# Lower halves of all expert-table blocks on VectorE, gathers paced by a one-column copy, first modulation columns turned in place

## Chip, core and metric

One core of a Trainium2 chip runs the whole program in one launch. The metric is the device time of that launch in microseconds (us). TensorE (PE), VectorE (DVE), ScalarE (ACT), GpSimd (POOL) and the queues of SyncE (SP) work side by side and wait for each other by semaphores.

## The reference, cut to what matters

Two layers, each a token mixer followed by a mixture of 16384 single-neuron experts ("PEER"). The mixture picks 16 experts for each of 8 heads of a token, by product keys:

```python
def peer_ffn(h, w_q, sub_keys, u_tab, v_tab):      # per block of 128 tokens
    s = einsum('thpd,hpnd->thpn', (xb @ w_q).reshape(t, 8, 2, 128), sub_keys)
    s_top, i_top = top_k(s, 16)
    c_top, c_idx = top_k(s_top[:, :, 0, :, None] + s_top[:, :, 1, None, :], 16)
    expert, gate = i1 * 128 + i2, softmax(c_top)
    act = gelu(einsum('td,thkd->thk', xb, u_tab[expert]))
    return einsum('thk,thkd->td', gate * act, v_tab[expert])
```

Before each mixer the input is normalized and modulated by a shift and a scale that come from one matrix product with `ada_w` (SEQ 512, context 256, D_MODEL 1024, float32 throughout).

## The kernel before, in words

**Two ways to the experts.** For three of the four tiles of 128 latent tokens (`ND = 3`, 384 tokens) the kernel works densely: all 16384 experts, in 128 blocks of 128 rows of each table, with a gate that is zero where an expert was not chosen (`peer_dense`, names `xp_` in layer 0, `yp_` in layer 1). For the fourth latent tile, and for the two context tiles of layer 0 (`cp_`), it fetches the chosen rows by indirect DMA from POOL, 128 rows of 4 KB a time (`gather_slots`, L1227), and DVE multiplies them: `jk` (L1245) for rows of `u`, `acc` (L1256) for rows of `v`. A gather needs one of six row buffers, and DVE's product gives it back. Layer 0 has 768 gathers, layer 1 has 256.

**Dense block.** Matrix products run in three passes on a rounded upper part and a remainder of each operand. For block b, SP loads `ur` (512 KB) and `vr` (512 KB), and every fourth block `gb` (768 KB of gates), each into two buffers. ACT rounds `ur` to `uh` (L1346) and `vr` to `vh` (L1384); the remainders `ul = ur - uh` (L1347) and `vl = vr - vh` are subtractions over 128x1024. PE forms the scores `sp` in 24 matmuls, ACT applies gelu (`ge`), DVE multiplies by the gates (`a`, L1394), ACT rounds to `ah`, DVE subtracts to `al` (L1399), and PE adds to the six accumulators `acc` in 18 matmuls. In program order the scores of block b stand ahead of the accumulation of block b-1.

**Who subtracts.** `ul` is on POOL for all 100 blocks that compute scores here. `vl` is on DVE for these (L1388) and on POOL for the last 28 (`FILL`, L1386), whose scores were computed earlier in the routing stage and are loaded as `gel`.

**Pacing.** `load(b)` ends with `pump(anchor, k)`: it writes the next k gathers into the program (3 a block in layer 0, 2.5 in layer 1, 2 in FILL) and puts each behind `anchor` on POOL. The anchor is the POOL subtraction of that block. Gathers and their products have the lowest priority, so a scheduler puts them where it expects idle time. In other stages `tick` (L1290) does the pacing: a copy of one column on POOL, which is then the anchor. What is left of the gathers after layer 0's dense stage is paced by ticks in layer 1's mixer and drained there.

**Start.** `ada` forms the modulation rows `ar`, writes them to memory (L179), `ada_cols(0)` reads them back as `ac_r` (L194), PE turns them in four transposes, and DVE copies the result to `cols` (L198), which ACT needs for the first normalized input `c_hT` (L235).

Of the kernel before, what the change touches and what calls it, by code (L numbers as in the profile page):

```python
# [9 lines left out]
F32 = mybir.dt.float32  # L10
# [9 lines left out]
P = 128  # L20
# [7 lines left out]
FILL = range(P - 28, P)  # L28
# [12 lines left out]
class Trunk:  # L41
# [114 lines left out]
    def ada(self, pool, layer, groups, ps):  # L156


        nc = self.nc
        for g in groups:  # L160
# [9 lines left out]
            b = pool.tile([P, 512], F32, tag="ab", name="ab" + nm)  # L170
            nc.sync.dma_start(b, self.I["ada_b"][layer, g])
            r = pool.tile([P, 512], F32, tag="ar", name="ar" + nm, bufs=2)
            nc.vector.tensor_add(r, acc, b)
            if g != 1:
# [14 lines left out]
    def ada_cols(self, layer):  # L189

        self.cols = self.rowpool.tile([P, 4, P], F32, tag="cols", name="cols")
        with self.tc.tile_pool(name=f"ac{layer}", bufs=1) as pool:
            r = pool.tile([P, 512], F32, name=f"ac_r{layer}")
            self.nc.sync.dma_start(r, self.rowd[layer][0])  # L194
            pt = self.ps("cols_ps")
            for b in range(4):
                self.tr(pt[:, b * P:(b + 1) * P], r[:, b * P:(b + 1) * P])
            self.nc.vector.tensor_copy(self.cols, pt)  # L198

# [1138 lines left out]
    def expert_scores(self, pool, b, xT, layer, nm, ps):  # L1338
# [7 lines left out]
        nc.scalar.copy(uh, uv)  # L1346
        anchor = nc.gpsimd.tensor_sub(ul, uv, uh)  # L1347

# [11 lines left out]
    def peer_dense(self, xs, xT, up, layer, nm, done):  # L1360
# [3 lines left out]
        with ExitStack() as st:  # L1364
# [4 lines left out]
            def load(b):  # L1369
# [95 lines left out]
    def build(self):  # L1465
        nc, tc, I = self.nc, self.tc, self.I
        with ExitStack() as st:
# [13 lines left out]
            with ExitStack() as l0:  # L1481
# [175 lines left out]
```

## Time and profile before

| | us |
|---|---|
| median of 3 runs (4374.13 to 4380.30) | 4376.23 |
| the profiled execution | 4360.89 |
| its span, first to last instruction | 4359.1 |
| PE busy | 3943.7 (90%) |
| DVE busy | 3497.9 (80%) |
| POOL busy | 2035.1 (47%) |
| layer 0, dense stage (first to last `sp`/`acc` matmul) | about 1553 to 2567 |
| layer 1, dense stage | about 3380 to 4342 |

The share of an engine over the whole span mixes stages with different limits, so the dense stages are read in windows: a stretch in which PE is busy for all its length is bound by PE, and only a stretch in which it is not can be shortened from outside. "Busy" for PE is a modelled end of a pipelined matmul; block times are therefore read from the start of one block's matmuls to the start of the next.

### The profile page before, as it was taken

To read this page: it belongs to the slowest core of one execution; us is meant where nothing else is said; L and a number is where in the kernel's file an instruction comes from. 1 tells how busy PE (TensorE), PEld (TensorE's weight loads), DVE (VectorE), ACT (ScalarE), POOL (GpSimd) and SP (SyncE) were. 2 spreads that over 40 slices of the span, in tenths; PEclk is the share of its full clock that TensorE was granted. 3 is DMA by queue.
4 is the path that set the end of the run, shared out by engine and by line. 5 is a ranking of instruction groups with operands and counts; after the bars stand their busy time and mean duration, and the time that the engine had idled before them with its cause. 6 is when DMAs were issued, how large, how long until landed. Compare 5 with 4: busy or idle time off the path is not lost.

```text
span 4359.1 us, 58568 instructions
## 1 busy us (share of the span) xinstructions
PE 3943.7 (90%) x20450; PEld 3198.6 (73%) x20450; DVE 3497.9 (80%) x6787; ACT 1613.3 (37%) x2929; POOL 2035.1 (47%) x1467
## 2 busy tenths in 40 slices
PE   7998888887799979999999865999999999999998
PEld 4676554685476767999999653775767899999986
DVE  1355989998899979999999977553998888888886
ACT  2353443353124523333333231562245333333333
POOL 0003367555630078767666856001200766666664
PEclk8999998998899989999999987999999999999999
DMA  8825498867934699999999978203246988888885
GB/s 305 295 105 158 166 323 315 279 222 242 316 118 159 227 365 353 346 344 352 337 345 332 325 260 301 67 26 103 73 161 232 346 317 308 309 305 312 309 287 178
DMA packets 484855, 1113.89 MB, mean 256 GB/s; under 512 B 38736, under 2 KB 256336, under 8 KB 475344
## 3 DMA queue, kind: packets, MB, share of 16 engines
q1 hardware_dynamic: 328896, 561.75, 37.4%
q0 software_dynamic: 147600, 537.40, 34.3%
q10 hardware_dynamic: 8064, 11.01, 0.7%
q8 instruction: 161, 2.64, 0.2%
q14 instruction: 134, 1.10, 0.1%
HBM read 1036.56 MB, written 73.92 MB: 255 GB/s over the span
## 4 chain that ended last, share of the span: by engine, by line
PE 61%; DVE 20%; DMA 8%; issue 6%; ACT 2%; POOL 2%; SPq 0%; DVEq 0%; ACTq 0%; POOLq 0%
PE yp_acc L75 10%; PE yp_sp L75 10%; PE xp_sp L75 9%; PE xp_acc L75 8%; PE mq_s L75 2%; DVE cp_acc L1256 2%; DMA cp_u<-peer_u,cp_idx 2%; PE x_p L75 1%; DVE cp_jk L1245 1%; PE yp_pg L75 1%; PE xp_pg L75 1%; DVE xp_acc L1256 1%; PE ada_ps L75 1%; PE yp_qy L75 1%; PE c_p L75 1%
## 5 line engine op out<-in xcount | busy, mean ns | idle before, releaser
L1227 POOL DMA_INDIRECT cp_u<-peer_u,cp_idx x256 | 318.0, 1242 | 316.0 <-DVE cp_jk L1245 222.6
L1347 POOL TENSOR_TENSOR yp_ul<-yp_ur,yp_uh 128x1024 fp32r<-128x1024 f32 x100 | 242.0, 2420 | 421.1 <-ACT yp_uh L1346 421.0
L75 PE MATMUL xp_sp<-xp_xT,xp_uh 128*128 128x384 f32 x1600 | 409.7, 337 | 12.4 <-ACT xp_uh L1346 12.4
L75 PE MATMUL yp_sp<-yp_xT,yp_uh 128*128 128x384 f32 x1600 | 408.8, 336 | 1.4 <-ACT yp_ge L1453 1.4
L1227 POOL DMA_INDIRECT cp_v<-peer_v,cp_idx x256 | 317.3, 1239 | 164.4 <-DVE cp_acc L1256 100.0
L75 PE MATMUL xp_acc<-xp_vh,xp_al 128*128 128x512 f32 x768 | 309.1, 402 | 31.9 <-DVE xp_al L1399 31.9
L1256 DVE SCALAR_TENSOR_TENSOR cp_acc<-cp_v,cp_act,cp_acc 128x1024 f32<-128x1024 f32 x254 | 330.9, 1303 | 6.9 <-DMA cp_v<-peer_v,cp_idx 4.4
L1394 DVE TENSOR_TENSOR yp_a<-yp_ge,yp_gb 128x384 f32<-128x384 f32 x100 | 237.3, 2373 | 123.3 <-ACT yp_ge L1356 123.3
L75 PE MATMUL xp_acc<-xp_vh,xp_ah 128*128 128x512 f32 x768 | 304.9, 397 | 15.8 <-ACT xp_ah L1398 15.8
L1347 POOL TENSOR_TENSOR xp_ul<-xp_ur,xp_uh 128x1024 fp32r<-128x1024 f32 x100 | 249.6, 2496 | 130.0 <-ACT xp_uh L1346 129.5
L75 PEld LDWEIGHTS xp_sp<-xp_xT,xp_uh 128*128 128x128 f32 x1600 | 293.2, 189 | 20.6 <-ACT xp_uh L1346 13.0
L75 PE MATMUL yp_acc<-yp_vh,yp_al 128*128 128x512 f32 x768 | 302.5, 394 | 5.5 <-DVE yp_al L1399 5.5
L75 PE MATMUL xp_acc<-xp_vl,xp_ah 128*128 128x512 f32 x768 | 304.8, 397 | 0.0
L75 PE MATMUL yp_acc<-yp_vl,yp_ah 128*128 128x512 f32 x768 | 301.6, 393 | 2.6 <-POOL yp_vl L1386 2.6
L75 PE MATMUL yp_acc<-yp_vh,yp_ah 128*128 128x512 f32 x768 | 299.9, 390 | 2.7 <-ACT yp_ah L1398 2.7
L75 PEld LDWEIGHTS yp_sp<-yp_xT,yp_uh 128*128 128x128 f32 x1600 | 292.4, 188 | 9.7 <-ACT yp_ge L1453 2.0
L75 PE MATMUL yp_sp<-yp_xT,yp_ul 128*128 128x384 f32 x800 | 269.4, 337 | 3.2 <-POOL yp_ul L1347 3.2
L75 PE MATMUL xp_sp<-xp_xT,xp_ul 128*128 128x384 f32 x800 | 269.8, 337 | 1.4 <-POOL xp_ul L1347 1.4
L1394 DVE TENSOR_TENSOR xp_a<-xp_ge,xp_gb 128x384 f32<-128x384 f32 x100 | 206.3, 2063 | 45.7 <-ACT xp_ge L1356 45.7
L1057 POOL TENSOR_TENSOR yp_wql<-yp_wq,yp_wqh 128x1024 fp32r<-128x1024 f32 x16 | 38.7, 2420 | 369.1 <-DMA yp_wq<-peer_w_q 311.5
L1346 ACT CAST yp_uh<-yp_ur 128x1024 fp32r<-128x1024 f32 x100 | 105.2, 1052 | 270.5 <-issue 214.7
L1398 ACT CAST xp_ah<-xp_a 128x384 fp32r<-128x384 f32 x128 | 65.8, 514 | 367.7 <-DVE xp_a L1394 323.5
(1479 smaller groups left out, 10753.1 us busy)
## 6 DMA issues: line engine op xcount, KB each, us to landing
xp_ur<-peer_uT SPq DMA_DIRECT2D x128, 512.0 KB, 5.7
xp_vr<-peer_v SPq DMA_DIRECT2D x128, 512.0 KB, 6.1
yp_ur<-peer_uT SPq DMA_DIRECT2D x128, 512.0 KB, 4.8
yp_vr<-peer_v SPq DMA_DIRECT2D x128, 512.0 KB, 4.9
aw<-ada_w SPq DMA_DIRECT2D x48, 1024.0 KB, 7.0
gdram<-xp_go SPq DMA_DIRECT2D x12, 2048.0 KB, 6.9
xp_gb<-gdram SPq DMA_DIRECT2D x32, 768.0 KB, 9.2
gdram<-yp_go SPq DMA_DIRECT2D x12, 2048.0 KB, 7.0
```

The lines of the kernel that those rows point to most:

```text
L75: self.nc.tensor.matmul(out, lhsT, rhs, start=start, stop=stop)
L1057: self.pump(nc.gpsimd.tensor_sub(wl, raw, wh), 0)
L1227: d = nc.gpsimd.indirect_dma_start(out=r, out_offset=None, in_=tab, in_offset=bass.IndirectOffsetOnAxis(ap=idx[:, j:j + 1], axis=0))
L1245: return nc.vector.scalar_tensor_tensor(junk, u, 1.0, h2, op0=ALU.mult, op1=ALU.mult, accum_out=act[:, j:j + 1])
L1256: i = nc.vector.scalar_tensor_tensor(acc, v, act[:, j:j + 1], acc, op0=ALU.mult, op1=ALU.add)
L1346: nc.scalar.copy(uh, uv)
L1347: anchor = nc.gpsimd.tensor_sub(ul, uv, uh)
L1394: nc.vector.tensor_mul(a.rearrange("p (g t) -> p g t", t=32), ge.rearrange("p (g t) -> p g t", t=32), gbs[b // 4][:, :, b % 4, :])
L1398: nc.scalar.copy(ah, a)
```

## The change

Three edits. Every `ul` and `vl` is subtracted on DVE. The gathers of the dense stage are paced by `tick(vh)`, a POOL copy of one column of the block's `vh`; it is written only while gathers are left. And the first modulation rows are turned by PE straight from `ar`, without the way through memory (the write to memory stays, other stages read it).

```diff
@@ ada
             nc.sync.dma_start(self.rowd[layer][g], r)
+            if not (layer or g):
+                self.turn_cols(r)
...
+    def turn_cols(self, r):
+        self.cols = self.rowpool.tile([P, 4, P], F32, tag="cols", name="cols")
+        pt = self.ps("cols_ps")
+        for b in range(4):
+            self.tr(pt[:, b * P:(b + 1) * P], r[:, b * P:(b + 1) * P])
+        self.nc.vector.tensor_copy(self.cols, pt)
@@ expert_scores
-        anchor = nc.gpsimd.tensor_sub(ul, uv, uh)
+        anchor = nc.vector.tensor_sub(ul, uv, uh)
@@ peer_dense, load
                 nc.scalar.copy(vh, vr)
-                if b in FILL:
-                    anchor = nc.gpsimd.tensor_sub(vl, vr, vh)
-                else:
-                    nc.vector.tensor_sub(vl, vr, vh)
-                self.pump(anchor, self.rate[layer] if b not in FILL else 2)
+                nc.vector.tensor_sub(vl, vr, vh)
+                self.tick(vh, self.rate[layer] if b not in FILL else 2)
                 return go, vh, vl
@@ build
                         weave(self.ada(ap, 0, (0,), self.ps))
-                        self.ada_cols(0)
```

POOL's queue in the first blocks of layer 0's dense stage, before: five gathers (`cp_u`) between the subtractions of blocks 6 and 7.

```order
L1347 TENSOR_TENSOR xp_ul6_12846<-xp_ur6_12843,xp_uh6_12845 128x1024
L1227 DMA cp_u1_109_12486<-peer_u0,cp_idx1_3839 128x1024
L1227 DMA cp_u1_110_12553<-peer_u0,cp_idx1_3839 128x1024
L1227 DMA cp_u1_111_12557<-peer_u0,cp_idx1_3839 128x1024
L1227 DMA cp_u1_112_12561<-peer_u0,cp_idx1_3839 128x1024
L1227 DMA cp_u1_113_12628<-peer_u0,cp_idx1_3839 128x1024
L1347 TENSOR_TENSOR xp_ul7_12921<-xp_ur7_12918,xp_uh7_12920 128x1024
```

The same place on POOL in the changed program, from the tick of block 6 to that of block 7.

```order
L1295 CAST tick_12861<-xp_vh6_12857 128x1
L1232 DMA cp_u1_109_12484<-peer_u0,cp_idx1_3833 128x1024
L1232 DMA cp_u1_110_12553<-peer_u0,cp_idx1_3833 128x1024
L1232 DMA cp_u1_111_12557<-peer_u0,cp_idx1_3833 128x1024
L1232 DMA cp_u1_112_12561<-peer_u0,cp_idx1_3833 128x1024
L1295 CAST tick_12938<-xp_vh7_12934 128x1
```

The subtraction has left POOL, and four gathers stand in a block where five stood; up to block 13 both programs place 56 gathers in the stage (1, 3, 1, 5, 4, 5, 5, 4, 5, 5, 4, 4, 5, 5 before; 4, 1, 4, 5, 4, 4, 4, 5, 4, 4, 4, 5, 4, 4 now), blocks 14 to 16 hold 4 or 3 of them before and 4 now, and from there on both have 3 a block.

DVE's queue in the middle of the stage, before: one block, from the gate product of block 41 to that of block 42.

```order
L1394 TENSOR_TENSOR xp_a41_15442<-xp_ge41_15440,xp_gb40_15328 128x384
L1256 SCALAR_TENSOR_TENSOR cp_acc1_13007<-cp_v1_101_15412,cp_act1_7245,cp_acc1_13007 128x1024
L1399 TENSOR_TENSOR xp_al41_15445<-xp_a41_15442,xp_ah41_15444 128x384
L1256 SCALAR_TENSOR_TENSOR cp_acc1_13007<-cp_v1_102_15478,cp_act1_7245,cp_acc1_13007 128x1024
L1256 SCALAR_TENSOR_TENSOR cp_acc1_13007<-cp_v1_103_15481,cp_act1_7245,cp_acc1_13007 128x1024
L1388 TENSOR_TENSOR xp_vl43_15547<-xp_vr43_15544,xp_vh43_15546 128x1024
L1394 TENSOR_TENSOR xp_a42_15514<-xp_ge42_15512,xp_gb40_15328 128x384
```

The same block on DVE in the changed program.

```order
L1396 TENSOR_TENSOR xp_a41_15520<-xp_ge41_15518,xp_gb40_15402 128x384
L1352 TENSOR_TENSOR xp_ul43_15621<-xp_ur43_15618,xp_uh43_15620 128x1024
L1401 TENSOR_TENSOR xp_al41_15523<-xp_a41_15520,xp_ah41_15522 128x384
L1390 TENSOR_TENSOR xp_vl43_15627<-xp_vr43_15624,xp_vh43_15626 128x1024
L1261 SCALAR_TENSOR_TENSOR cp_acc1_13019<-cp_v1_101_15490,cp_act1_7239,cp_acc1_13019 128x1024
L1261 SCALAR_TENSOR_TENSOR cp_acc1_13019<-cp_v1_102_15558,cp_act1_7239,cp_acc1_13019 128x1024
L1261 SCALAR_TENSOR_TENSOR cp_acc1_13019<-cp_v1_103_15561,cp_act1_7239,cp_acc1_13019 128x1024
L1396 TENSOR_TENSOR xp_a42_15594<-xp_ge42_15592,xp_gb40_15402 128x384
```

The subtraction `ul` of the block after next stands between `a` and `al`, where a gather's product stood, and all three products now stand in a row ahead of the next block's `a`.

DVE's queue in layer 0's FILL blocks, before: from the gate product of block 106 to that of block 107.

```order
L1394 TENSOR_TENSOR xp_a106_20056<-xp_gel106_20042,xp_gb104_19968 128x384
L1256 SCALAR_TENSOR_TENSOR xp_acc0_19312<-xp_v0_26_19934,xp_act0_16076,xp_acc0_19312 128x1024
L1256 SCALAR_TENSOR_TENSOR xp_acc0_19312<-xp_v0_27_19937,xp_act0_16076,xp_acc0_19312 128x1024
L1399 TENSOR_TENSOR xp_al105_20021<-xp_a105_20018,xp_ah105_20020 128x384
L1394 TENSOR_TENSOR xp_a107_20094<-xp_gel107_20080,xp_gb104_19968 128x384
```

And in the changed program.

```order
L1396 TENSOR_TENSOR xp_a106_20264<-xp_gel106_20248,xp_gb104_20170 128x384
L1261 SCALAR_TENSOR_TENSOR xp_acc0_19494<-xp_v0_25_20099,xp_act0_16172,xp_acc0_19494 128x1024
L1261 SCALAR_TENSOR_TENSOR xp_acc0_19494<-xp_v0_26_20136,xp_act0_16172,xp_acc0_19494 128x1024
L1401 TENSOR_TENSOR xp_al105_20227<-xp_a105_20224,xp_ah105_20226 128x384
L1390 TENSOR_TENSOR xp_vl106_20253<-xp_vr106_20250,xp_vh106_20252 128x1024
L1396 TENSOR_TENSOR xp_a107_20304<-xp_gel107_20288,xp_gb104_20170 128x384
```

`vl` has come to DVE, behind `al`. Over the 28 FILL blocks POOL's queue holds 47 gathers now where it held 56, and the 9 others stand behind the last tick, ahead of layer 1's mixer. In layer 1's FILL blocks both programs hold six.

## Rows read from the trace of the kernel before

**Rows 1.** Windows: length, busy us (instructions) of each engine, PE clock, DMA share, GB/s.

```profile
1550.00:1700.00 150.00, 129.19 (x606) 111.28 (x607) 137.25 (x148) 44.54 (x62) 129.24 (x78) 0.96 0.98 357
1700.00:2400.00 700.00, 700.00 (x3541) 637.26 (x3540) 653.84 (x640) 244.72 (x338) 506.70 (x337) 1.00 0.94 342
2404.00:2567.00 163.00, 133.77 (x525) 104.19 (x524) 154.01 (x113) 42.78 (x57) 138.06 (x83) 0.93 0.94 322
3450.00:4200.00 750.00, 750.00 (x3795) 683.00 (x3795) 637.41 (x610) 263.47 (x363) 476.84 (x318) 1.00 0.86 308
4211.00:4296.00 85.00, 77.00 (x324) 61.10 (x323) 58.20 (x54) 29.07 (x41) 47.65 (x23) 0.98 0.77 261
```

**Rows 2.** Chain that ended last: start, us, what; dense stage of layer 0.

```profile
1553.28 6.52 PE xp_sp L75 x22
...
1693.36 4.18 PE xp_sp L75 x24
1697.54 4.12 PE xp_acc L75 x18
```

**Rows 3.** Tiles: operation, count, duration in ns (min/median/max), first and last start.

```profile
L1347 POOL TENSOR_TENSOR xp_ul<-xp_ur,xp_uh x100: 2364/2400/3348, 1550.9 to 2388.0; 128x1024 fp32r<-128x1024 f32 x100
...
L1384 ACT CAST xp_vh<-xp_vr x128: 1042/1048/1057, 1535.3 to 2558.0; 128x1024 fp32r<-128x1024 f32 x128
L1388 DVE TENSOR_TENSOR xp_vl<-xp_vr,xp_vh x100: 1210/1219/3460, 1538.3 to 2395.0; 128x1024 fp32r<-128x1024 f32 x100
...
L1399 DVE TENSOR_TENSOR xp_al<-xp_a,xp_ah x128: 542/547/2754, 1562.0 to 2566.1; 128x384 fp32r<-128x384 f32 x128
L1394 DVE TENSOR_TENSOR xp_a<-xp_ge,xp_gb x100: 543/2470/2762, 1560.4 to 2404.2; 128x384 f32<-128x384 f32 x100
...
L1290 POOL COPY tick<-x_p x32: 182/335/1272, 498.6 to 673.3; 128x1 f32<-128x1 f32 x32
```

**Rows 4.** DVE by line, 1560 to 2395: busy, mean ns | idle before.

```profile
L1256 DVE SCALAR_TENSOR_TENSOR xp_acc<-xp_v,xp_act,xp_acc 128x1024 f32<-128x1024 f32 x15 | 19.1, 1275 | 0.2
```

**Rows 5.** Timeline of POOL, then of DVE, one early block of layer 0.

```profile
1600.66 2.41 POOL L1347 TENSOR_TENSOR xp_ul<-xp_ur,xp_uh 128x1024 fp32r<-128x1024 f32 x1
...
1611.77 2.42 POOL L1347 TENSOR_TENSOR xp_ul<-xp_ur,xp_uh 128x1024 fp32r<-128x1024 f32 x1
...
1600.74 3.43 DVE L1245 SCALAR_TENSOR_TENSOR cp_jk<-cp_u,c_o1h 128x1024 bf16<-128x1024 f32 x1 [0.90 <-DMA cp_u<-peer_u,cp_idx]
```

**Rows 6.** DMA: rate in 40 slices of 1550:1700; landings in 2404:2567 and 4210:4296.

```profile
GB/s 345 326 288 365 370 295 265 366 419 411 409 411 343 386 402 407 409 380 306 301 307 320 310 313 370 405 411 403 370 314 334 387 320 335 281 368 411 404 406 317
...
xp_vr<-peer_v SPq DMA_DIRECT2D x25, 512.0 KB, 6.2
...
yp_vr<-peer_v SPq DMA_DIRECT2D x17, 512.0 KB, 4.8
```

**Rows 7.** Waits (us, times, longest): FILL of layer 0, of layer 1, and DVE 1560:2395.

```profile
PE xp_acc L75 <- DVE xp_al L1399: 29.2, 16, 4.0
...
SPq L1377 <- POOL yp_vl L1386: 46.1, 17, 6.4
...
DVE cp_jk L1245 <- DMA cp_u<-peer_u,cp_idx: 6.9, 8, 2.9
```

**Rows 8.** Timeline of the start.

```profile
38.96 0.47 SPq L194 DMA_DIRECT2D ac_r<-row  x1
...
40.52 2.19 ACT L230 ACTIVATE c_x<-c_x,c_r 128x1024 f32<-128x1024 f32 x2 [1.02 <-DVE c_r L128]
43.68 0.72 PEld L78 LDWEIGHTS cols_ps<-ident,ac_r 128*128 128x128 f32 x4 [10.43 <-DMA ac_r<-row]
...
45.63 3.76 ACT L235 ACTIVATE c_hT<-c_hT,cols 128x256 f32<-128x256 f32 x8 [2.92 <-DVE cols L198]
```

**Rows 9.** Timeline of DVE and POOL behind layer 0's dense stage.

```profile
2584.91 0.17 DVE L119 TENSOR_SCALAR mc_v<-mc_ssq 128x2 f32<-128x2 f32 x1 [10.34 <-ACT mc_sqj L219]
...
2604.81 0.18 POOL L1290 COPY tick<-m_psb 128x1 f32<-128x1 f32 x1 [37.86 <-ACT m_psb L83]
```

More of the change, by code (lines that the diff above doesn't have):

```diff
@@ L189, in ada_cols @@
     def ada_cols(self, layer):
-        self.cols = self.rowpool.tile([P, 4, P], F32, tag="cols", name="cols")
         with self.tc.tile_pool(name=f"ac{layer}", bufs=1) as pool:
@@ L194, in ada_cols @@
             self.nc.sync.dma_start(r, self.rowd[layer][0])
[L195 to L198, printed above, removed]
+            self.turn_cols(r)
+    def turn_cols(self, r):
[4 more added lines that the diff above has]
+        self.nc.vector.tensor_copy(self.cols, pt)
     def mod_col(self, half, kb, s):
```

## The prediction

> **What bounds the kernel now.** I read the windows first, stage by stage, then the chain of waits inside the stages in which PE is not full, and last the durations of single operations.
>
> In the long middle of both dense stages PE is busy for the whole window: 700 of 700 us in layer 0 and 750 of 750 us in layer 1, at clock 1.00 [rows 1]. A block there is 24 score matmuls (4.18 us) and 18 accumulating ones (4.12 us), 8.30 us in all [rows 2]. Nothing that leaves POOL or comes to DVE can shorten these 1450 us; it can only lengthen them.
>
> PE falls short in three stretches that the change touches. The head of layer 0: the scores of block 0 start at 1553.28 and those of block 14 at 1693.36, so 14 blocks take 140.1 us where 14 x 8.30 = 116.2 would do; 24 us are lost. Layer 0's FILL blocks: 525 matmuls, 29.2 blocks of 18, in 163 us, 5.58 us a block against 4.12 [rows 1]; at 4.12 they would need 120 us, so 43 us are lost. Layer 1's FILL blocks: 324 matmuls, 18 blocks, in 85 us against 74 us [rows 1]; 11 us are lost. With the start this is some 80 us that can be had at all.
>
> What is late there is a lock between POOL and DVE. A gate product `a` takes 0.54 us at the least and 2.47 us in the median, and the POOL subtraction beside it 2.40 us; `al` takes 0.55 us in the median but up to 2.75 us [rows 3]. In the head a gather's product that starts 0.08 us after a POOL subtraction takes 3.43 us [rows 5], against 1.28 us for such a product [rows 4]. So while POOL subtracts, DVE stands in an instruction, about 2 us for each. On POOL itself the head's block is full: from one subtraction to the next are 11.1 us [rows 5], filled by five gathers and the subtraction. In layer 0's FILL, PE's longest wait is for `al` [rows 7], and DVE is busy for 154 of 163 us [rows 1].
>
> **The change, part by part.** Durations are those of the profiled execution, 4360.9 us; it lies 15.3 us under the median of 4376.2. The gains are put on the median.
>
> *Middle of the stages.* DVE gains a `ul`, which I price as the `vl` of the same shape, 1.22 us [rows 3], and loses the lock, 2.47 - 0.55 = 1.92 us. Its new block is three products 3 x 1.28, `a` 0.55, `al` 0.55, `ul` 1.22, `vl` 1.22: 7.38 us of 8.30, in layer 1 with 2.5 products 6.74. PE's 8.30 us hide it, and `ul` is written two blocks ahead of its scores. Room is 0.92 us a block, less the tick. Cost 0. POOL gives up 2.40 us a block and gets a tick, 0.34 us in the median [rows 3]. Behind the tick stand the block's gathers, behind these the products on DVE; the tick waits for `vh`, which ACT casts a block ahead. POOL then works 5 to 6 us of 8.30, so that wait costs nothing.
>
> *Head of layer 0.* POOL's block falls from 11.1 us to four gathers and a tick: 11.1 - 2.4 = 8.7 for five gathers, four fifths of it 7.0, with the tick 7.3 us. DVE's is 4 x 1.28 + 3.54 = 8.66 us, in 14 blocks 121 us. DMA carries the same 56 gathers of 0.524 MB and 14 times 0.524 + 0.524 + 0.196 MB of tables and gates, 46.8 MB: 131 us at the window's mean of 357 GB/s, 114 us at the 410 GB/s of its better slices [rows 1, 6]. Bounds: 116.2 us (PE) and 140.1 us (nothing gained). I take 127 us, between DVE's 121 and DMA's 131, since both press at once. Blocks 14 to 16 now carry four gathers and not three or four; DVE's 8.66 against 8.30 costs 1.3 us at most. Gain 140.1 - 127 - 1.3 = 11.8 us, bounds 0 and 24.
>
> The Trainium skill weighs in here. The page "DMA: Bandwidth & Descriptors", section "Specifications", puts the limit of memory for one core at about 358 GB/s. By it the head can't go under 46.8 / 0.358 = 131 us, and the gain would be 7.8 us. The trace differs: single slices of this window move 402 to 419 GB/s [rows 6], so I do not take it as a wall.
>
> *FILL of layer 0.* Before, DVE's block is two products 2.55, `a` 0.55 and `al` 0.55, plus about 2 us of lock: 5.6 us, which is the time of the block. Now POOL subtracts nothing, and DVE's block is 47/28 = 1.68 products of 1.28, `a`, `al`, and `vl` 1.22: 4.47 us. Next is the loop of the two `vr` buffers: landing 6.2 us [rows 6], cast 1.05 us, `vl` 1.22 us [rows 3], 8.5 us for two blocks or 4.2 us each, and more where `vl` stands behind a product. DMA: 322 GB/s x 163 us = 52.5 MB before, less 9 gathers 47.8 MB, 1.64 MB a block: 5.08 us at 322 GB/s and 4.58 us at 357. I take 4.9 us, nearer to the rate seen in this very stretch: 29.2 x 4.9 = 143 us. Gain 20 us; bounds 4.5 (DVE) and 5.3 (DMA, with a wait), which give 32 and 8 us.
>
> *Behind it.* Nine gathers move behind the last tick. POOL stood idle there for 37.9 us, until the mixer's first tick, and DVE 10.3 us before `mc_v` [rows 9]; five products of 1.28 us fit in that. But four others now stand ahead of the last multiplications `dy`, and the gathers run beside the reload of the latent tiles. Cost 3 us, bounds 0 and 8 (half of 9 x 0.524 MB at 322 GB/s).
>
> *FILL of layer 1.* SP's loads of `vr` wait 46.1 us for POOL's `vl` [rows 7]. The loop is landing 4.8, cast 1.05, `vl` 2.4: 8.3 us for two blocks, 4.1 each, exactly PE's pace with nothing to spare; with `vl` at 1.22 it is 3.5. Six gathers remain there. Of the 11 us I take 6 back, since `gel` and the last tile's own output stay; bounds 0 and 10.
>
> *Start.* `ac_r` was issued at 38.96, its transposes started at 43.68, and ACT's `c_hT` at 45.63 [rows 8]. `ar` was in memory before that load, so its transposes and the copy to `cols` now end near 41 at the latest, and `c_hT` waits for the scaled `c_x`, which ends at 40.52 + 2.19 = 42.7; with a transpose behind it, 43.0. Gain 2.6 us, bounds 0 and 3.
>
> Sum: 11.8 + 20 - 3 + 6 + 2.6 = 37 us. Time 4376 - 37 = 4339 us.
>
> **Rivals.**
>
> *DMA is the next bound throughout.* For it: DMA share 0.98 in the head and 0.94 in FILL [rows 1]. Head at 131 us, gain 7.8; FILL at 5.08 us a block, 148 us, gain 15; behind it -8; layer 1 3, start 2. Together 20 us: 4357 us. The skill's page above would favour this one. Against it: the 410 GB/s slices.
>
> *The tick takes what the subtraction gave back.* A tick lasts up to 1.27 us [rows 3]. If each held DVE for so long, DVE's block in layer 0's middle would be 7.38 + 1.27 = 8.65 us, 0.35 us over PE's, times 84 blocks (700 / 8.30) 29 us: 4368 us. Layer 1 has 6.74 + 1.27, still under 8.30. Against it: the median tick is 0.34 us. The skill's page "SBUF — State Buffer", section "Who interferes with whom", supports the mechanism: a DVE instruction with two inputs in SBUF and a POOL instruction that reads SBUF shut each other out, and the tick reads SBUF. The trace agrees that the lock exists (2.47 against 0.55 us), not that a tick is long.
>
> *Slower: DVE's queue is held by late rows.* Three products now stand in a row ahead of `a`, `ul`, `al` and `vl`. If the rows come late, all four wait, and PE behind them. With 0.92 - 0.34 = 0.58 us of room a block, a wait of 1.0 us in each of 84 blocks eats the 37 us; a wait of one whole product, 1.28 us, costs (1.28 - 0.58) x 84 = 59 us: 4398 us. Against it: for rows of the first table DVE waited 8 times, 6.9 us, in the stretch up to 2395 [rows 7], and six buffers let gathers run a block ahead.
>
> *PE is the next bound everywhere*: head 24, FILL 32, behind it 0, layer 1 10, start 2.6, together 68: 4308 us. It needs 400 GB/s for long.
>
> *The lock was not the cause.* The blocks of head and FILL keep their time because landings set it, and only 5 us from start and layer 1 remain: 4371 us. Against it: DVE's 154 of 163 us.
>
> **How the numbers follow.** Forecast 0.54, DMA 0.20, tick 0.06, slower 0.08, PE 0.07, lock not the cause 0.05. A measurement here can tell about 0.2%, 8.8 us. Faster by more: 0.54 + 0.20 + 0.07 = 0.81; within it (4368 and 4371): 0.11; slower: 0.08. The range leaves out PE's 4308 and the slower case, 0.15 together: 4312 to 4372.
>
> **What would show it.** In the changed profile `a` should be near 0.55 us and `ul` near 1.22 us on DVE; PE full in both middles at 8.30 us a block; 14 head blocks in 127 us; FILL of layer 0 at 4.9 us a block with DVE no longer full; `c_hT` starting near 43. The forecast is wrong if PE waits for `al` or `ul` in the middle, if DVE waits for gathered rows there, or if FILL keeps 5.6 us a block with DMA at its old rate.

## Result and the profile after

The changed kernel takes 4328.53 us (median of 4 runs, 4318.16 to 4335.68) against 4375.18 us before (4374.01 to 4380.30): ratio 0.9892, 95% interval 0.9878 to 0.9906. That is 46.7 us less, where 37 us were forecast. The profiled execution took 4335.68 us, its span is 4333.9 us, only 25.2 us under the span before: the execution of before that was profiled (4360.89 us) was faster than any of the timed ones, the one of after was the slowest of its four. A pair of profiles from one chip, below (e0_both and e1_start), is therefore the better comparison of stretches.

Windows of the changed kernel that answer to [rows 1], same columns: head, middle and FILL of layer 0, middle and FILL of layer 1.

```profile
1557.00:1707.00 150.00, 142.85 (x691) 127.93 (x692) 132.52 (x175) 50.79 (x70) 100.91 (x82) 0.96 1.02 384
1707.00:2393.00 686.00, 685.96 (x3468) 624.10 (x3468) 581.18 (x713) 246.15 (x330) 413.93 (x333) 1.00 0.97 344
2394.00:2537.00 143.00, 130.91 (x542) 102.89 (x540) 119.17 (x136) 41.66 (x57) 98.46 (x78) 0.96 0.97 346
3430.00:4180.00 750.00, 750.00 (x3789) 687.00 (x3788) 581.25 (x698) 270.20 (x361) 399.10 (x317) 1.00 0.90 308
4190.00:4275.00 85.00, 80.05 (x342) 64.56 (x341) 56.23 (x76) 30.05 (x43) 7.21 (x8) 0.98 0.84 274
```

Both middles stay full for PE, and DVE is lighter there than before (581 of 686 us), although it now does every `ul`. In FILL DVE has fallen from 154 of 163 us to 119 of 143, and the transfers have risen from 322 to 346 GB/s. The tiles that answer to [rows 3] say why (operation, count, min/median/max ns, first and last start):

```profile
L1352 DVE TENSOR_TENSOR xp_ul<-xp_ur,xp_uh x100: 1215/1218/1226, 1557.3 to 2380.1; 128x1024 fp32r<-128x1024 f32 x100
L1401 DVE TENSOR_TENSOR xp_al<-xp_a,xp_ah x128: 547/551/559, 1566.9 to 2532.0; 128x384 fp32r<-128x384 f32 x128
L1396 DVE TENSOR_TENSOR xp_a<-xp_ge,xp_gb x100: 547/552/559, 1565.3 to 2394.9; 128x384 f32<-128x384 f32 x100
L1295 POOL COPY tick<-xp_vh x128: 181/1168/2022, 1543.5 to 2529.7; 128x1 f32<-128x1 f32 x128
```

`a` is at 0.55 us without one exception (median 2.47 before), `al` no longer reaches 2.75 us, and `ul` costs DVE the 1.22 us that it was priced at. The tick is another matter: 1.17 us in the median, not 0.34.

The head (chain of waits; start, us, what). Before, 140.1 us passed from the scores of block 0 to those of block 14 [rows 2].

```profile
1557.31 1.24 DVE xp_ul L1352
1558.59 6.18 PE xp_sp L75 x22
...
1677.53 11.34 DMA cp_v<-peer_v,cp_idx
...
1689.06 1.22 DVE xp_vl L1390
1690.28 1.21 DVE cp_acc L1261
...
1700.05 4.18 PE xp_sp L75 x24
1704.24 4.12 PE xp_acc L75 x18
1708.36 4.18 PE xp_sp L75 x24
```

The timeline puts block 14's first score matmul at

```profile
1680.50 0.33 PE L75 MATMUL xp_sp<-xp_xT,xp_uh 128*128 128x384 f32 x1
```

so 14 blocks took 1680.50 - 1558.59 = 121.9 us. A window of these blocks (columns as in [rows 1]) and the longest wait in it:

```profile
1558.60:1680.50 121.90, 117.29 (x568) 105.89 (x569) 107.27 (x150) 41.45 (x56) 80.54 (x67) 0.95 1.03 385
...
ACT xp_uh L1351 <- DMA xp_ur<-peer_uT: 31.3, 8, 10.2
```

DVE is busy for 107 of the 121.9 us and not full; the transfers move 385 GB/s, and ACT waits for tables `ur`. The two blocks behind them took 19.55 us instead of 16.6 (block 16 starts at 1700.05): a gathered row landed after 11.34 us, and `vl` stood on DVE behind its product. From there on a block takes 8.30 us.

FILL of layer 0, waits (us, times, longest), against [rows 7]:

```profile
ACT xp_vh L1389 <- DMA xp_vr<-peer_v: 72.4, 23, 8.8
...
PE xp_acc L75 <- DVE xp_al L1401: 7.2, 7, 1.6
```

PE waited 29.2 us for `al` before and waits 7.2 us now. ACT waited for `vr` before too (66.2 us), but in the chain of waits through this stretch the products and `al` on DVE held 48% of the time before, and now the landing of `vr` holds 39%. About 30 blocks (542 matmuls, 18 a block) in 143 us are 4.8 us a block.

The seam, as the stretch from the last `al` to layer 1's `mc_v` is called here (DVE's timeline: start, us, operation), against [rows 9]:

```profile
2532.02 0.55 DVE L1401 TENSOR_TENSOR xp_al<-xp_a,xp_ah 128x384 fp32r<-128x384 f32 x1
2532.49 5.24 DVE L1261 SCALAR_TENSOR_TENSOR xp_acc<-xp_v,xp_act,xp_acc 128x1024 f32<-128x1024 f32 x4
2537.64 1.28 DVE L1434 TENSOR_TENSOR xp_dy<-xp_acc,xp_dg 128x512 f32<-128x512 f32 x2
...
2544.90 6.55 DVE L1261 SCALAR_TENSOR_TENSOR xp_acc<-xp_v,xp_act,xp_acc 128x1024 f32<-128x1024 f32 x5
2561.93 0.17 DVE L119 TENSOR_SCALAR mc_v<-mc_ssq 128x2 f32<-128x2 f32 x1 [10.48 <-ACT mc_sqj L224]
```

Four products stand between the last `al` and `dy`, and from `al` to `mc_v` pass 29.9 us; before they were 2584.91 - 2566.1 = 18.8 us [rows 3, 9]. From `al` to `dy` are 5.6 us, before 1.1 (`dy` started at 2567.19). The transfers in the chain there, the last store of an output tile (`x`) and the reload of a context tile (`mc_x`), of the changed kernel (start, us, what),

```profile
2547.34 5.41 DMA x<-xp_dx
2553.13 7.54 DMA mc_x<-c
```

and of the kernel before, at the same place:

```profile
2574.60 4.02 DMA x<-xp_dx
...
2578.64 3.73 DMA mc_x<-c
```

The store was also issued later: its data were complete at 2544.98, but SP stood in the load before it, which waited for the first output tile to land (timeline of the changed kernel):

```profile
2540.20 2.72 SPq L1529 DMA_DIRECT2D x<-xp_dx  x2
...
2546.98 0.32 SPq L112 DMA_DIRECT2D mx_x<-x  x1
2547.34 0.43 SPq L1529 DMA_DIRECT2D x<-xp_dx  x1
```

From the first store to that load are 6.8 us here; before they were 3.1 (2569.81 to 2572.86), and the last store went out at 2574.60, when its data were complete.

### The profile page after: what moved, and what is told of

Its sections match the earlier page's. It is cut to its first block, busy times and chain, and to the rows that moved or that the text cites. A ratio compares the mean times of both kernels' runs of the same rounds, so it can differ in the third digit from the quotient of the medians.

```text
span 4333.9 us, 58682 instructions
## 1 busy us (share of the span) xinstructions
PE 3942.1 (91%) x20450; PEld 3207.5 (74%) x20450; DVE 3328.7 (77%) x7043; ACT 1626.7 (38%) x2929; POOL 1720.3 (40%) x1443
## 3 DMA queue, kind: packets, MB, share of 16 engines
q0 software_dynamic: 147600, 537.40, 35.2%
## 4 chain that ended last, share of the span: by engine, by line
PE 60%; DVE 19%; DMA 11%; issue 5%; ACT 2%; POOL 2%; SPq 0%; ACTq 0%; DVEq 0%; POOLq 0%
PE yp_acc L75 11%; PE yp_sp L75 10%; PE xp_sp L75 9%; PE xp_acc L75 8%; PE mq_s L75 2%; DVE cp_acc L1261 2%; DMA xp_vr<-peer_v 1%; DMA xp_ur<-peer_uT 1%; PE yp_pg L75 1%; PE xp_pg L75 1%; DVE cp_jk L1250 1%; DMA cp_u<-peer_u,cp_idx 1%; PE x_p L75 1%; PE c_p L75 1%; PE yp_qy L75 1%
## 5 line engine op out<-in xcount | busy, mean ns | idle before, releaser
L1232 POOL DMA_INDIRECT cp_v<-peer_v,cp_idx x256 | 328.0, 1281 | 171.2 <-DVE cp_acc L1261 103.8
L1295 POOL COPY tick<-yp_vh 128x1 f32<-128x1 f32 x104 | 117.9, 1134 | 520.9 <-ACT yp_vh L1389 520.9
L75 PEld LDWEIGHTS xp_sp<-xp_xT,xp_uh 128*128 128x128 f32 x1600 | 293.1, 189 | 19.9 <-ACT xp_uh L1351 12.2
L1390 DVE TENSOR_TENSOR yp_vl<-yp_vr,yp_vh 128x1024 fp32r<-128x1024 f32 x128 | 156.7, 1224 | 151.3 <-ACT yp_vh L1389 151.2
L1390 DVE TENSOR_TENSOR xp_vl<-xp_vr,xp_vh 128x1024 fp32r<-128x1024 f32 x128 | 156.7, 1224 | 105.5 <-ACT xp_vh L1389 104.2
L1295 POOL COPY tick<-xp_vh 128x1 f32<-128x1 f32 x128 | 138.8, 1084 | 246.3 <-ACT xp_vh L1389 245.8
L1351 ACT CAST xp_uh<-xp_ur 128x1024 fp32r<-128x1024 f32 x100 | 105.3, 1053 | 275.4 <-PE xp_sp L75 213.9
L1389 ACT CAST xp_vh<-xp_vr 128x1024 fp32r<-128x1024 f32 x128 | 134.5, 1051 | 174.5 <-PE xp_acc L75 87.9
```

What stands on the lines that cost most here:

```text
L75: self.nc.tensor.matmul(out, lhsT, rhs, start=start, stop=stop)
L1232: d = nc.gpsimd.indirect_dma_start(out=r, out_offset=None, in_=tab, in_offset=bass.IndirectOffsetOnAxis(ap=idx[:, j:j + 1], axis=0))
L1295: self.pump(self.nc.gpsimd.tensor_copy(t, src[:, 0:1]), k)
```

## Experiments

Eleven experiments ran, each with a profile. This table gives the length of each stretch in us, read from first and last starts: to the first scores of layer 0; to the first product `a` with a `gel`; to the last `al` (FILL 0); to `mc_v` (seam); to the first scores of layer 1 (mixer and routing); to its first `gel` product; to its last `al` (FILL 1); the last 21.7 us, from the last `al` of layer 1 to the end, are left out (22.0 in n_notick; 23.7 in p_poolsub and 26.7 in v_vr3, which have two buffers for the output tiles in place of three). One profile stands behind each row, so a few us of a difference between two rows can be scatter; the medians can tell more.

| kernel | median | start | head, middle 0 | FILL 0 | seam | mixer | middle 1 | FILL 1 |
|---|---|---|---|---|---|---|---|---|
| before | 4375.2 | 1550.8 | 853.9 | 161.4 | 18.8 | 793.4 | 833.3 | 125.8 |
| changed | 4328.5 | 1557.3 | 838.0 | 136.7 | 29.9 | 796.5 | 832.3 | 121.5 |
| e0_both | 4331.9 | 1559.4 | 835.0 | 136.9 | 30.5 | 795.8 | 830.8 | 116.8 |
| e1_start | 4376.3 | 1561.0 | 853.0 | 163.4 | 19.8 | 794.2 | 834.7 | 127.6 |
| e2_fill | 4351.9 | 1556.3 | 855.7 | 138.4 | 29.6 | 794.6 | 835.6 | 116.8 |
| e3_ul | 4358.5 | 1557.1 | 836.4 | 163.1 | 23.2 | 794.3 | 832.7 | 124.9 |
| r1_fill1 | 4353.7 | 1555.1 | 840.5 | 127.4 | 21.5 | 835.9 | 831.9 | 116.2 |
| r2_325 | 4318.5 | 1560.6 | 840.0 | 129.9 | 19.8 | 801.5 | 832.5 | 115.9 |
| r3_350 | 4296.7 | 1555.0 | 858.0 | 128.6 | 20.9 | 765.3 | 831.6 | 117.8 |
| h_half | 4306.0 | 1535.0 | 829.0 | 154.6 | 19.9 | 793.8 | 831.6 | 118.6 |
| p_poolsub | 4395.8 | 1556.6 | 837.5 | 176.5 | 32.5 | 796.3 | 830.3 | 142.6 |
| v_vr3 | 4329.1 | 1554.7 | 834.9 | 136.6 | 35.2 | 793.7 | 829.9 | 115.9 |
| n_notick | 4323.2 | 1556.7 | 837.9 | 143.5 | 29.1 | 795.1 | 825.7 | 117.3 |

**e0_both.** The changed kernel, no edit.

> The changed kernel itself, on the same chip as the three kernels that carry one part of the change each. In its first profile the span is 25.2 us shorter than before, while the medians differ by 46.7 us; by marks of the two traces the head of layer 0 gave 15.9 us, the FILL blocks of layer 0 24.6 us, the FILL blocks of layer 1 4.9 us, the stretch between the dense stage and layer 1's first gel took 13.1 us back, and 6.5 us more had passed before the first scores of layer 0. Theory: the 6.5 us ahead of the dense stage are scatter of single executions, not the change; a second profile then shows the first scores of layer 0 within 2 us of where the kernel with the start alone has them, and the time is 4376 - 37 to - 47 us. Rival: the changed program is slower ahead of the dense stage; the first scores stand again some 6 us later than in a kernel without the new dense stage.

Ratio 0.9899 (0.9885 to 0.9914), 4331.86 us against 4377.12. The first scores stand at 1559.4; in e2_fill and e3_ul, whose code up to there is that of before, at 1556.3 and 1557.1, in e1_start at 1561.0. Only the first profile of before had 1550.8. So the 6.5 us ahead of the dense stage are scatter of executions, as the theory said. Of the profiles from this chip e1_start is the one that can stand for before (its median is that of before): its span is 48.5 us longer than that of e0_both.

**e1_start.** The start edit alone.

```diff
+            if not (layer or g):
+                self.turn_cols(r)
...
-                        self.ada_cols(0)
```

> The kernel before with the start alone changed: the first modulation columns are turned straight from ar. Theory: c_hT starts 2.35 us earlier relative to ar (10.58 us behind it before, 8.23 us in the changed kernel) and the whole program ends 2.4 us earlier: ratio 0.9995. Rival: the stage that follows waits for its weights, the lead is gone by about 110 us (the last c_v was 0.4 us early in the changed kernel), and the time is that of before, within 1 us. No measurement here can tell 2.4 us from nothing; the marks in the trace can.

Ratio 1.0003 (0.9994 to 1.0012): nothing, as the rival said. In the trace the lead is there and melts. The first `c_q` matmul starts at 46.1 us here, at 48.9 and 48.6 in e2_fill and e3_ul; the last `c_v` at 110.5 against 113.0 and 111.7; `cp_xT` at 367.6 against 366.7 and 367.0. Part of it goes into waits of PE for transfers of modulation weights (`aw`) up to 370 us: 6.7 us here, 5.3 in e2_fill. The rest was not traced.

**e2_fill.** `vl` of the FILL blocks alone.

```diff
-                if b in FILL:
-                    anchor = nc.gpsimd.tensor_sub(vl, vr, vh)
-                else:
-                    nc.vector.tensor_sub(vl, vr, vh)
-                self.pump(anchor, self.rate[layer] if b not in FILL else 2)
+                nc.vector.tensor_sub(vl, vr, vh)
+                if b in FILL:
+                    self.tick(vh, 2)
+                else:
+                    self.pump(anchor, self.rate[layer])
```

> The kernel before with only the lower parts vl of the 28 FILL blocks on VectorE, and the gathers of these blocks behind a tick; ul stays on POOL in the 100 blocks that compute scores. 47 gathers in layer 0's FILL blocks where 54 stood, nine behind the last tick. Theory (the lock in FILL is worth what the prediction said, the seam more): FILL of layer 0 -20 to -25 us, behind it +3 to +14, FILL of layer 1 -5: together -10 to -25 us, ratio 0.994 to 0.998; FILL at 4.8 to 4.9 us a block. Rival (landings set FILL, the lock is not its cause): 5.4 us a block or more, ratio 0.999 to 1.000.

Ratio 0.9943 (0.9930 to 0.9956), 25 us. FILL 0 has about the changed kernel's length (138.4), the seam its cost (29.6), the head that of before. FILL also lost seven gathers to the seam by this edit; they are not the gain, since p_poolsub below keeps them out as well and has no gain.

**e3_ul.** `ul` of the 100 blocks alone.

```diff
-        anchor = nc.gpsimd.tensor_sub(ul, uv, uh)
+        anchor = nc.vector.tensor_sub(ul, uv, uh)
...
                 if b in FILL:
                     anchor = nc.gpsimd.tensor_sub(vl, vr, vh)
+                    self.pump(anchor, 2)
                 else:
                     nc.vector.tensor_sub(vl, vr, vh)
-                self.pump(anchor, self.rate[layer] if b not in FILL else 2)
+                    self.tick(vh, self.rate[layer])
```

> The kernel before with only the lower parts ul of the 100 blocks that compute scores on VectorE, their gathers behind a tick; the FILL blocks keep vl on POOL as anchor, and 54 gathers. Theory: the head gives 12 to 16 us, the middle nothing (PE full at 8.30 us a block), FILL keeps 5.5 us a block, nothing is given back behind it: -12 to -16 us, ratio 0.996 to 0.997. Rival (the tick, 1.17 us in the median of the dense stage, takes what the subtraction gave back): the head keeps about 10 us a block and the ratio is 0.999 to 1.001.

Ratio 0.9961 (0.9947 to 0.9974), 18.6 us, a little over the 12 to 16 expected; the seam gave 3 us back (23.2 against 19.8 in e1_start), which was not expected and was not traced. The two parts lie in different places, as two windows of each show; e2_fill first, head and FILL 0:

```profile
1557.00:1707.00 150.00, 133.57 (x628) 115.45 (x628) 140.85 (x150) 43.73 (x63) 131.51 (x80) 0.96 0.97 359
2412.00:2555.00 143.00, 129.65 (x536) 101.35 (x534) 117.51 (x135) 40.80 (x56) 102.79 (x77) 0.98 0.97 342
```

then e3_ul:

```profile
1557.00:1707.00 150.00, 143.81 (x701) 128.66 (x702) 134.32 (x176) 50.64 (x70) 102.67 (x83) 0.97 1.03 390
2394.00:2557.00 163.00, 134.54 (x513) 102.73 (x512) 149.50 (x112) 41.42 (x56) 137.23 (x80) 0.92 0.93 317
```

With `ul` off POOL PE does 701 matmuls in the head's 150 us, with it on POOL 628. The three parts add up: 0.9 + 25.3 + 18.6 = 44.8 us of e0_both's 45.3.

**p_poolsub.** The lock by itself: POOL subtracts into a tile that no engine reads.

```diff
                 nc.vector.tensor_sub(vl, vr, vh)
-                self.tick(vh, self.rate[layer] if b not in FILL else 2)
+                if b in FILL:
+                    vx = r3.tile([P, D], F32R, tag="vx", name=nm + f"_vx{b}", bufs=1)
+                    self.pump(nc.gpsimd.tensor_sub(vx, vr, vh), 2)
+                else:
+                    self.tick(vh, self.rate[layer])
...
-                    x = tp.tile([P, D], F32, tag="x", name=nm + f"_dx{t}", bufs=3)
+                    x = tp.tile([P, D], F32, tag="x", name=nm + f"_dx{t}", bufs=2)
```

> The changed kernel with one operation added in each FILL block: POOL subtracts vr - vh a second time into a tile that nobody reads, and this takes the tick's place ahead of the gathers. DVE's queue is that of the changed kernel. (The output tiles of the dense stage have two buffers for x in place of three.) Theory (the lock): a and al beside the POOL subtraction lengthen again from 0.55 to over 2 us, DVE's FILL block becomes 4.5 + 2 = 6.5 us or, where products or vl meet it, somewhat less; FILL of layer 0 5.5 to 6.5 us a block, 15 to 45 us slower than the changed kernel. Rival (it was the late result of POOL's subtraction that held PE, not a lock): nobody waits for this result, so FILL stays at 4.8 us a block.

4395.78 us, ratio 1.0043 (1.0029 to 1.0057), slower than before the change. A window of its FILL 0:

```profile
2394.00:2574.00 180.00, 138.90 (x523) 103.30 (x522) 175.52 (x134) 42.74 (x56) 140.49 (x76) 0.93 0.79 272
```

Two blocks of it (timeline: start, us, operation):

```profile
2470.32 3.97 DVE L1390 TENSOR_TENSOR xp_vl<-xp_vr,xp_vh 128x1024 fp32r<-128x1024 f32 x1
...
2470.79 2.42 POOL L1393 TENSOR_TENSOR xp_vx<-xp_vr,xp_vh 128x1024 fp32r<-128x1024 f32 x1
...
2477.27 4.21 POOL L1393 TENSOR_TENSOR xp_vx<-xp_vr,xp_vh 128x1024 fp32r<-128x1024 f32 x1
2477.55 1.22 DVE L1390 TENSOR_TENSOR xp_vl<-xp_vr,xp_vh 128x1024 fp32r<-128x1024 f32 x1
...
2479.15 3.41 DVE L1261 SCALAR_TENSOR_TENSOR xp_acc<-xp_v,xp_act,xp_acc 128x1024 f32<-128x1024 f32 x1
```

No engine reads `vx`, yet `vl` takes 3.97 us, a product 3.41, and DVE is full again (176 of 180 us) at 6.2 us a block. It falls on `vl` (2.53 us in the mean of the FILL blocks, 1.22 in the changed kernel) and the products (1.54 against 1.28) rather than on `a` and `al`, whose medians stay at 0.55 us; that part of the expectation was wrong. In the first block DVE stands until POOL is done; in the second POOL stands in `vx` while `vl` runs its 1.22 us, and then the product stands. That is the lock, and with it the rival falls: the lengthened instructions are DVE's own. The next load into `vr` does have to wait for `vx` to have read it, but SP stood for that only 11.0 us, against 97.6 us for `vl`. The whole cost, 64 us against e0_both, is more than expected: layer 0's FILL grew by 39.6 us, and layer 1's, which the expectation had left out, by 25.8; the missing output buffer takes 2 us at the seam and 2 at the end.

**n_notick.** The tick taken away; POOL's and DVE's orders stay.

```diff
-                nc.vector.tensor_sub(vl, vr, vh)
-                self.tick(vh, self.rate[layer] if b not in FILL else 2)
+                anchor = nc.vector.tensor_sub(vl, vr, vh)
+                self.pump(anchor, self.rate[layer] if b not in FILL else 2)
```

> The changed kernel without the 232 ticks of the dense stages: the gathers keep their order on POOL, DVE keeps its order, and only the six row buffers and DVE's products hold a gather back. Theory (the tick costs nothing: POOL stands in it, DVE does not): the same time within 8 us, a stretch of the middle full for PE, vl and ul at 1.22 us. Rival 1 (the ticks, 257 us of POOL in all, hold the gathers): faster by over 10 us, in head and FILL. Rival 2 (the ticks keep the gathers from running ahead of the tables): the head slower, ur landing later.

4323.15 us, ratio 0.9889 (0.9871 to 0.9907), span 4327.3 us against 4326.9 for e0_both: in the whole the tick costs nothing, and rival 1 falls. So does rival 2 for the head, whose 14 blocks, from the first score matmul on, took 122.4 us in this profile and 121.4 in e0_both. FILL 0 was 6.6 us longer, though, and the four profiles with ticks and as many gathers lie between 136.6 and 138.4; whether the tick's pacing helps there is open, with one profile.

**v_vr3.** A third buffer for `vr`.

```diff
-                vr = r3.tile([P, D], F32, tag="vr", name=nm + f"_vr{b}")
+                vr = r3.tile([P, D], F32, tag="vr", name=nm + f"_vr{b}", bufs=3)
...
-                    x = tp.tile([P, D], F32, tag="x", name=nm + f"_dx{t}", bufs=3)
+                    x = tp.tile([P, D], F32, tag="x", name=nm + f"_dx{t}", bufs=2)
```

> The changed kernel with three buffers for vr instead of two (and two instead of three for the output tiles x, which cost 2 us at the seam and 2 us at the end in the kernel with the discarded subtraction). Every engine's order is that of the changed kernel. Theory (the loop of landing, cast and vl over two buffers holds the FILL blocks, and SP's queue stands behind it): FILL of layer 0 from 137 to 120 to 128 us. Rival (the rate of the transfers holds them): 47.8 MB stay, and FILL keeps 133 us or more (47.8 MB at 354 GB/s are 135 us). In the head, where ACT waits 31 us for ur and not for vr, no change.

FILL 0 took 136.6 us, as the rival said. ACT's wait for `vr` fell from 66.0 us in e0_both to 21.8, and others took its place (waits, 2400 to 2520; e0_both, then v_vr3):

```profile
ACT xp_vh L1389 <- DMA xp_vr<-peer_v: 66.0, 21, 7.5
```

```profile
ACT xp_vh L1389 <- DMA xp_vr<-peer_v: 21.8, 10, 7.1
...
DVE xp_a L1396 <- DMA xp_gel<-gedram: 18.0, 8, 6.3
PE xp_acc L75 <- DVE xp_al L1401: 15.3, 8, 6.2
```

The `gel` load is now the late one. So the loop of the two buffers does not set FILL. What all transfers need together is the likely limit: r1_fill1 below, which takes 20 gathers out of FILL, does shorten it. But it takes their products off DVE with them, so the transfers are not shown by themselves.

**h_half.** Each product over half of the columns (`junk`, `u`, `h2` and `acc`, `v` cut to `[:, :512]`); the other half is left out. One execution, 4306.0 us.

> The changed kernel with each gather's product taken over 512 of the 1024 columns (the rows are fetched whole, half of each product is left out): a product takes about 0.65 us in place of 1.28, DVE's FILL block about 3.4 to 3.6 us, the bytes that are moved are the same or more (54 gathers in FILL instead of 47). Theory (transfers hold the FILL blocks of the changed kernel): FILL of layer 0 stays at 4.7 to 5.0 us a block. Rival (DVE still holds them): it falls to PE's 4.12 to 4.3 us a block. For the head the same: with transfers as its limit it stays near 8.9 us a block.

FILL 0 became longer, 154.6 us, which neither side expected:

```profile
2364.00:2518.00 154.00, 132.17 (x510) 103.17 (x509) 98.50 (x139) 41.33 (x56) 87.81 (x80) 0.89 0.94 334
```

DVE was busy for only 98.5 of 154 us and waited 44.3 us for `vh` behind the landing of `vr`. The scheduler, given shorter products, had put 54 gathers into FILL and `vl` ahead of `al` on DVE, so that `al` stood behind a late table. DVE's load was not the limit of this FILL; the run does not size the transfers, because two things changed. The head missed the expectation too: 14 blocks, from the first score matmul on, took 116.7 us, 8.3 a block and PE's own pace, not 8.9. But it held 39 gathers and not 53, at 357 GB/s, so what holds the changed kernel's head at 121.9 us, the transfers or the products, is not separated by any run here.

**r1_fill1.** One gather a FILL block.

```diff
-                self.tick(vh, self.rate[layer] if b not in FILL else 2)
+                self.tick(vh, self.rate[layer] if b not in FILL else 1)
```

> The changed kernel with one gather a block in the FILL blocks where it had two: 27 gathers beside layer 0's FILL instead of 47, 1 behind the last tick instead of 9, no gather's product ahead of the last multiplications dy; 41 gathers instead of 13 stand behind the last tick of layer 1's mixer. Theory A (FILL of the changed kernel is held by transfers, vr landing 7 us; the seam's 10 us are the nine gathers and their products): FILL of layer 0 from 136.9 to about 125 us (4.3 us a block), last al to mc_v from 30.5 back to 19.8 us, the 28 gathers moved into the mixer cost between 0 and 28 x 1.28 = 36 us of DVE there; between 4310 and 4345 us. Theory B (the loop of the two vr buffers sets FILL whatever else is moved): FILL stays at 4.7 us a block or more.

4353.7 us, ratio 0.9948 (0.9931 to 0.9964), slower than the range of theory A, whose first two parts came: FILL 0 127.4 us, seam 21.5.

```profile
2396.00:2523.00 127.00, 119.61 (x508) 95.58 (x507) 92.77 (x111) 41.49 (x56) 65.52 (x54) 0.99 0.89 297
```

FILL falls to 4.5 us a block with the transfers at 297 GB/s. The 28 gathers cost more than DVE's 36 us in the mixer: 835.9 against 795.8, 40.1 us. DVE's products there, by lines (count, busy us, mean ns, idle before), in e0_both from 2620 to 2720:

```profile
L1261 DVE SCALAR_TENSOR_TENSOR xp_acc<-xp_v,xp_act,xp_acc 128x1024 f32<-128x1024 f32 x38 | 48.7, 1281 | 7.8 <-DMA xp_v<-peer_v,xp_idx 7.3
```

and in r1_fill1 from 2600 to 2720:

```profile
L1261 DVE SCALAR_TENSOR_TENSOR xp_acc<-xp_v,xp_act,xp_acc 128x1024 f32<-128x1024 f32 x67 | 85.9, 1282 | 14.7 <-DMA xp_v<-peer_v,xp_idx 13.5
```

A gather left over for the mixer costs 40.1 / 28 = 1.43 us, more than its product of 1.28: none of it is hidden.

**r2_325 and r3_350.** The middle of layer 0 takes more gathers, besides the edit of r1_fill1.

```diff
-        self.rate = (3, 2.5)
+        self.rate = (3.25, 2.5)      # r2_325
+        self.rate = (3.5, 2.5)       # r3_350
```

> The changed kernel with 3.25 gathers a block in the middle of layer 0 where it had 3, and one in FILL where it had two: 286 gathers in blocks 14 to 99 instead of 261, 27 in FILL instead of 47, 1 behind the last tick instead of 9, 16 behind the mixer's last tick instead of 13. DVE's middle block becomes 7.38 + 0.25 x 1.28 = 7.70 us of 8.30, the transfers 343 + 0.25 x 0.524 MB / 8.30 us = 359 GB/s, both under what the head sustained (387 GB/s). Theory: the middle stays full for PE, FILL falls to about 125 us, the seam goes back by 10 us: some 20 us faster than the changed kernel, 4305 to 4315 us. Rival: the middle has no room for more (landings of ur or late rows hold DVE), it grows by 0.2 us a block or more, 17 us, and nothing is left.

> The changed kernel with 3.5 gathers a block in the middle of layer 0 and one in FILL: 311 gathers in blocks 14 to 99 (261 in the changed kernel, 286 at 3.25), 27 in FILL, 1 behind the last tick, and none left behind the last tick of layer 1's mixer, where 13 (16 at 3.25) stood. DVE's middle block becomes 7.38 + 0.5 x 1.28 = 8.02 us of 8.30; transfers 343 + 0.5 x 0.524 MB / 8.30 us = 375 GB/s, under the 387 of the head. Theory: the middle stays full but for a few us (838 to 845 us from the first scores to the first gel product, 840 at 3.25), FILL 127 to 130 us, seam 20 us, and the mixer gets shorter by 13 to 16 products of 1.28 us, from 796 to 780 - 785 us: 4295 to 4310 us. Rival: DVE's 0.28 us of room are not enough beside late rows; the middle grows by 0.3 us in each of 86 blocks, 26 us: 4320 us or more.

At 3.25: 4318.45 us, ratio 0.9862 (0.9846 to 0.9879), 3 us above the range; seam and FILL as expected, but the mixer has three gathers more and takes 5.7 us more; the middle, 840.0 us, lies within the scatter of the kernels at rate 3 (834.9 to 840.5). At 3.5: 4296.71 us, ratio 0.9831 (0.9817 to 0.9845), the best of all. The total was expected, the parts were not. The rival's middle came true, 858 us, some 20 more than at 3. The mixer more than paid for it with 30.5 us less than in e0_both: the expectation had counted the 13 gathers behind its last tick, but in the whole mixer stand 30 here and 52 in the changed kernel, 22 fewer at 1.39 us. By the number of gathers in the mixer (30, 52, 55 and 80) it takes 765.3, 795.8, 801.5 and 835.9 us, close to a straight line. A window of the middle of r3_350:

```profile
1700.00:2400.00 700.00, 686.04 (x3423) 613.62 (x3422) 626.53 (x753) 234.34 (x327) 473.39 (x378) 1.00 1.00 369
```

and two of its waits (1707 to 2400; us, times, longest):

```profile
DVE xp_jk L1250 <- DMA xp_u<-peer_u,xp_idx: 33.5, 30, 2.6
ACT xp_uh L1351 <- DMA xp_ur<-peer_uT: 30.9, 10, 6.7
```

In the changed kernel these two waits were 4.9 and 1.5 us (1707 to 2393). At 369 GB/s, DMA share 1.00, rows and tables come late: here is what the forecast's slower rival described, at 3.5 gathers a block and not at 3.

## Why the prediction was right, step by step

The stretches, changed kernel less before in us, from the first pair of profiles and from the pair of one chip (e0_both less e1_start; there the start is in both):

| step | forecast | first pair | one chip |
|---|---|---|---|
| up to layer 0's first scores | -2.6 | +6.5 | -1.6 |
| head and middle of layer 0 | -11.8 | -15.9 | -18.0 |
| FILL of layer 0 | -20 | -24.7 | -26.5 |
| behind it, to `mc_v` | +3 | +11.1 | +10.7 |
| mixer and routing | 0 | +3.1 | +1.6 |
| middle of layer 1 | 0 | -1.0 | -3.9 |
| FILL of layer 1 | -6 | -4.3 | -10.8 |
| sum | -37 | -25.2 | -48.5 |

- **What bounds the kernel, the lock: right.** `a` and `al` fell to 0.55 us in every block, and p_poolsub brings 3 to 4 us instructions back with a subtraction whose result no engine reads. "The lock was not the cause" is excluded.
- **Middle at no cost: right**, PE 685.96 of 686 us. The tick behind it was mis-sized, 1.17 us in the median against 0.34, and it did not matter: it is POOL that stands in it. The rival of the tick had the length nearly right (1.27) and the bearer wrong; n_notick shows no price.
- **Head: mechanism right, size short.** 14 blocks took 121.9 us, not 127. The term that was mis-sized is the transfers' 131 us, and with it the value between 121 and 131: they moved 46.9 MB in these blocks, the 46.8 of the forecast, but at 385 GB/s where 357 had been taken. That 121.9 lies so near to DVE's 121 does not make DVE the limit: it was busy for 107 us of it, and 53 products ran there, not 56. The Trainium skill, "DMA: Bandwidth & Descriptors", section "Specifications", has about 358 GB/s as the limit of memory for one core. The measurement decides: this one core, running alone, exceeds it, with 384 GB/s over 150 us. Of the gain, 3 us came back in blocks 14 to 16 (1.3 expected), by a late row ahead of `vl`.
- **FILL of layer 0: right in size a block (4.8 us, 4.9 forecast)** and in what comes next, the transfers, as far as v_vr3 and r1_fill1 show it. The gain is 25 us and not 20: from the first `a` with a `gel` to the last, 27 blocks, 150.6 us became 131.1, which is the forecast (4.86 us a block); 5 us more lie in the last block, from whose `a` to whose `al` 10.7 us passed before and 5.6 now, and which the sum did not have.
- **Behind it: the term that failed.** Forecast 3 us with bounds 0 and 8, measured 11. The forecast let five products hide in the 10.3 us ahead of `mc_v`, and priced the gathers beside the reload too low. In the trace the five do hide, but the other four, 5.2 us, stand between `al` and `dy` and cost 4.5 us; and the transfers behind them are slower beside the gathers, which is the larger part: the last store goes out 2.4 us late behind a slow first one, and `x` and `mc_x` land 5.4 and 7.5 us after their release, 4.0 and 3.7 before. (Of the kernel before, too, two gathers stood behind POOL's last subtraction, so the seam has seven more and not nine.) r1_fill1 moves eight of the nine away and the seam is back at 21.5.
- **FILL of layer 1:** forecast 6; with `vl` on DVE it takes 116 to 121.5 us, with it on POOL 124.9 to 127.6. The 10 us that were the bound are about reached in the pair of one chip, not in the first pair (4.3).
- **Start: the step failed at its last link.** `c_hT` starts 2.4 us earlier behind `ar` (8.2 against 10.6 us), but the stage behind it does not keep the lead; e1_start measures nothing.
- **Sum.** By the pair of one chip the head and the two FILLs were 17.5 us too small, the seam 7.7 us too cheap, and the rest nearly cancels; 37 came near the measured 46.7 in part by luck, by two errors of opposite sign.

## What to carry over

A two-input subtraction on POOL beside two-input operations on DVE was paid for twice in this kernel: price it as DVE time, by comparing the same DVE instruction with and without POOL beside it. When work is moved out of a stretch, follow it to where it lands: here a gather costs nothing measurable in the PE-bound middle up to 3.25 a block, 1.4 us in the mixer and over 1 us at the seam. So leftovers belong into the stage that is bound by another engine. Even where rows began to come late this paid: at 3.5 a block the middle lost some 20 us and the mixer gained 30.

## Not expected of the hardware

A POOL copy of one column, 0.18 us at the least, lasts until the DVE subtraction that it meets is done, and DVE does not lengthen. A block in the middle of layer 0 of the changed kernel (timeline: start, us, operation):

```profile
1818.06 1.23 DVE L1390 TENSOR_TENSOR xp_vl<-xp_vr,xp_vh 128x1024 fp32r<-128x1024 f32 x1 [1.17 <-ACT xp_vh L1389]
1818.16 1.17 POOL L1295 COPY tick<-xp_vh 128x1 f32<-128x1 f32 x1 [2.52 <-ACT xp_vh L1389]
```

`vl` ends at 1819.29, the copy at 1819.33. Both wait for the same `vh`, so they often start together; over all 128 blocks no `al` or `a` exceeds 0.56 us and no `vl` 1.23. The Trainium skill, "SBUF — State Buffer", section "Who interferes with whom", says that the one that is issued first keeps the port for its whole instruction and the other waits. The block above agrees, and so do 99 more of the 128: the copy starts behind `vl` and ends with it. A few blocks do not agree by their recorded starts; this one stands at the end of FILL 0:

```profile
2529.66 1.29 POOL L1295 COPY tick<-xp_vh 128x1 f32<-128x1 f32 x1 [0.24 <-ACT xp_vh L1389]
2529.69 1.22 DVE L1390 TENSOR_TENSOR xp_vl<-xp_vr,xp_vh 128x1024 fp32r<-128x1024 f32 x1
```

Here the copy has the earlier start and is still the one that lasts, to 2530.95, when `vl` ends at 2530.91; a product was running on DVE when it started. In p_poolsub's first block above, the other way round, `vl` has the earlier start (2470.32 against 2470.79) and is the one that stands. So either a recorded start is not the moment at which the port is taken, or more than the order of issue decides. No run here tells which.
